# The new-state product of the second mixer from high and low parts, time-step tiles in shared places, and the streams' sums over their scaled x

## The chip, the cores and the metric

The kernel runs on one core of a Trainium2 chip. The metric is the device time of one execution in microseconds. Three runs of the kernel before gave a median of 2522.05 us (2519.87 to 2525.16).

## What is computed

One inference step of a two-layer streaming encoder in float32, for two groups of requests that share the weights: one new stream of 512 frames (the prompt) and 8 running streams of 16 frames each. Together these are 640 tokens of 1024 features. Layer 0 is a half-step feed-forward block, a mixer (S5 and attention) and a feed-forward block. Layer 1 is the same around a Mamba-2 mixer, the "second mixer", which is where the change is. Its core, from the reference:

```python
def step(h, inp):
    x_c, dt_c, b_c, c_c = inp
    cs = jnp.cumsum(dt_c * a, axis=1)
    seg = cs[:, :, None] - cs[:, None]
    decay = jnp.exp(jnp.where(causal, seg, -jnp.inf))
    cb = jnp.einsum('btgn,bsgn->btsg', c_c, b_c)
    w = cb[..., None] * decay * dt_c[:, None]
    y = jnp.einsum('btsgr,bsgrp->btgrp', w, x_c)
    y = y + jnp.einsum('btgn,bgrpn->btgrp', c_c, h) * jnp.exp(cs)[..., None]
    to_end = jnp.exp(cs[:, -1:] - cs) * dt_c
    h_new = h * jnp.exp(cs[:, -1])[..., None, None] + jnp.einsum('bsgr,bsgn,bsgrp->bgrpn', to_end, b_c, x_c)
    return h_new, y
```

There are 4 groups of 8 heads; a head has 64 values and a state of 64x128. The last einsum is the new-state product: over the tokens of a chunk, B (128 state columns) with x scaled by `to_end` (512 columns: 8 heads of 64). The result is gated by silu(z), normalised per group and multiplied by the output weights.

## The kernel before

The program runs six phases one after the other (two feed-forward blocks around each mixer). Nearly all large products are made from float32 weights that are split into two fp32r tiles, a high part (ScalarE, which the profile calls ACT, casts; L101) and a low part (VectorE, DVE, subtracts; L102), by the helper `split`. A product is then three fp32r matmuls, high·high, high·low and low·high (helper `mm3`, L148). Weights that are scaled too come from L127 and L128. A few small products of the mixers are plain F32 matmuls. A framework orders the instructions of each engine when the program is built, by priorities and by when tiles of its pools come free; the order on an engine is fixed from then on. Tiles of one name share `bufs` places in SBUF; a tile with a name takes the next place as soon as its last reader is done.

The second mixer holds the tokens in five chunks of 128: c = 0 to 3 for the prompt, c = 4 for the 8x16 stream tokens. It first computes the time steps (tiles `dt` and `cs`, 32 rows by 640 tokens; `cs` is written to `cs_d` in DRAM) and the first group's inputs. Then it goes through 20 steps (g, c), groups in order, c in the order 4, 0, 1, 2, 3. Around step i stand:

- `core_a` of step i + 1: loads `bx` (B, C and four blocks of x of one chunk, 384 KB, two places, L1682) and `csb` (L1687), builds the decays (`csb`, L1709 to L1717), the product C·B (L1713), transposes B (L1714, copied to `bk` by ACT at L1720) and x (L1723), and scales x twice per head: `xe` by `to_end` times dt (for the state) and `xd` by dt (for y). In group 3 `xd` comes from DVE (L1727), all else from ACT (L1731). For c = 4 it also splits `xe` and `bk` into high and low parts (into a place of the pool of `h0`, in group 0 into that of `og`, and into `bs`) and stores them to `xb_d`, for a later phase.
- `core_b` (c < 4): C times the old state (L1749), the new-state product `pst` from `bk` and `xe` (L1753, one F32 matmul of 128x512), the new state `hst` (L1759), the weighted sum (L1767, eight F32 matmuls, one for each head, from `xd` and `csb`), and y (L1771, L1772 and four instructions of L1774, which read `bx` last and so free its place). For c = 0 there is no old state.
- `core_s` (c = 4): the streams' sums (L1786), the streams' states `h0` (four loads of 512 KB for a group, L1478, four places) times C (L1791), and their sum over `xe` (L1793, L1794), which is transposed (L1797) and added to x (L1800).
- one or two fills: a projection with its convolution (`xbc`, L1600 to L1609) or a gate (`gate_in`, L1621 to L1627) of the next group, with 512 KB weight loads at L120; after the third group there are none left.
- `gate_out` of the group before: loads `zz` (L1815), gates (L1816), sums squares (L1820, L1821), normalises (L1823, L1824), splits into `og` and projects (L148 with `og`), adding to `yacc` (L1832).

In groups 0 to 2 the projections of the next group fill the engines between the steps. The last group's steps have none; after them comes the gate of group 3 with the normalisation. SP issues all these loads and stores in its own fixed order.

## Time and profile before

| | |
|---|---|
| median of three runs | 2522.05 us (2519.87 to 2525.16) |
| profiled execution, its own time | 2521.54 us |
| span of its trace | 2519.8 us |
| TensorE (PE) busy | 2480.4 us (98%) |
| DVE busy | 2013.5 us (80%) |
| ACT busy | 1269.7 us (50%) |
| POOL busy | 376.8 us (15%) |
| granted TensorE clock, mean | 0.999 |
| steps of the second mixer | about 1656 to 2046 us of the span |

A page line such as `L148 PE MATMUL bank<-w,og 128*128 128x512` names the source line, the engine, the operation, the tile written and the tiles read, and the shape. `bank` is a PSUM bank. A wait is written behind an instruction as `[1.71 <-DMA bx<-bcx_d]`: the engine stood idle for 1.71 us before it, until that transfer was in. An F32 matmul appears as two records; an fp32r matmul as one. Lines that issue a DMA carry the engine SPq, and the time there is that of the issue, not of the transfer. Starts are counted from the span's beginning.

### The profile page before, as it was taken

The page shows a single profiled execution, that of the slowest core. Times are in us where ns is not written, and L with a number is a line of the kernel's source. Part 1 is how long each engine was busy: PE and PEld are TensorE (multiplying, and loading weights), DVE is VectorE, ACT ScalarE, POOL GpSimd, SP SyncE. Part 2 cuts the span into 40 slices and gives each one's busy share as a digit, 9 for nine tenths or more (in the row PEclk, how much of TensorE's full clock was granted, in tenths as well). Part 3 has the DMA queues.
Part 4 walks back from the last instruction along what each step waited for, and adds up shares of the span by engine and source line. Part 5 has one row for each costly group of instructions (what it writes and reads, how often), then busy time and mean ns, then how long its engine had stood idle before and what let it go on. Part 6 is the DMA issues. An engine that isn't in the chain of part 4 may idle for free. (4 is left out here: it accounts for less than half of the span.)

```text
span 2519.8 us, 40822 instructions
## 1 busy us (share of the span) xinstructions
PE 2480.4 (98%) x15559; PEld 2278.3 (90%) x15559; DVE 2013.5 (80%) x3507; ACT 1269.7 (50%) x2390; POOL 376.8 (15%) x493
## 2 busy tenths in 40 slices
PE   9999999999999999999999999999999999999998
PEld 8999999878789999999999999998989879999897
DVE  8788777666879888877988887777576789998887
ACT  4443344336744555553455554566565543554542
POOL 0000001210130000013000002311121162111121
PEclk9999999999999999999999999999999999999999
DMA  5332335443221433462144434456464723555563
GB/s 187 109 101 86 108 118 156 145 154 122 79 84 59 121 101 99 111 165 66 59 114 113 121 101 132 152 163 210 139 215 135 244 74 100 159 147 166 150 174 116
DMA packets 178085, 324.80 MB, mean 129 GB/s; under 512 B 21296, under 2 KB 90928, under 8 KB 177376
## 3 DMA queue, kind: packets, MB, share of 16 engines
q1 hardware_dynamic: 164032, 293.83, 36.4%
q0 software_dynamic: 13856, 28.35, 5.8%
q8 instruction: 122, 2.00, 0.3%
q14 instruction: 75, 0.61, 0.1%
HBM read 259.56 MB, written 40.54 MB: 119 GB/s over the span
## 5 line engine op out<-in xcount | busy, mean ns | idle before, releaser
L101 ACT CAST w<-raw 128x512 fp32r<-128x512 f32 (+1 forms) x721 | 532.7, 769 | 333.9 <-DVE raw L370 145.1
L102 DVE TENSOR_TENSOR w<-raw,w 128x512 fp32r<-128x512 f32 (+2 forms) x721 | 621.3, 883 | 84.7 <-ACT w L101 81.6
L387 PE MATMUL bank<-xhi,w 128*128 128x320 f32 x2432 | 436.0, 309 | 2.2 <-DVE s L429 1.4
L387 PE MATMUL bank<-T,w 128*128 128x320 f32 x2736 | 428.0, 309 | 5.4 <-ACT bank L404 2.8
L387 PEld LDWEIGHTS bank<-T,w 128*128 128x128 f32 x2736 | 406.8, 188 | 8.4 <-ACT bank L404 5.3
L387 PEld LDWEIGHTS bank<-xhi,w 128*128 128x128 f32 x2432 | 376.8, 188 | 6.1 <-DVE s L429 2.2
L148 PE MATMUL bank<-xhi,w 128*128 128x256 f32 (+2 forms) x2272 | 361.3, 310 | 5.0 <-DVE yacc L1832 1.4
L148 PEld LDWEIGHTS bank<-xhi,w 128*128 128x128 f32 x2272 | 334.3, 187 | 15.0 <-issue 3.7
L148 PE MATMUL bank<-w,h 128*128 128x512 f32 (+1 forms) x1500 | 346.5, 389 | 0.2 <-DVE yacc L234 0.2
L148 PEld LDWEIGHTS bank<-w,h 128*128 128x128 f32 x1500 | 277.8, 188 | 57.6 <-ACT h L101 1.6
L387 PE MATMUL bank<-xlo,w 128*128 128x320 f32 x1216 | 227.7, 309 | 0.0
L370 DVE TENSOR_TENSOR raw<-raw 128x512 f32<-128x512 f32 x304 | 211.7, 696 | 3.4
L387 PEld LDWEIGHTS bank<-xlo,w 128*128 128x128 f32 x1216 | 190.7, 188 | 0.0
L148 PE MATMUL bank<-xlo,w 128*128 128x256 f32 (+2 forms) x1136 | 189.8, 308 | 0.0
L536 POOL DMA_DIRECT2D yacc<-ev x84 | 72.7, 890 | 690.7 <-ACT ev L535 608.8
L148 PEld LDWEIGHTS bank<-xlo,w 128*128 128x128 f32 x1136 | 170.9, 187 | 0.6
L523 PE MATMUL bank<-w,h 128*128 128x512 f32 x576 | 134.5, 389 | 0.0
L523 PEld LDWEIGHTS bank<-w,h 128*128 128x128 f32 x576 | 107.8, 188 | 22.8
L400 ACT COPY mx<-bank 128x320 f32<-128x320 f32 x152 | 64.5, 425 | 105.4 <-PE bank L387 105.0
L234 DVE SCALAR_TENSOR_TENSOR yacc<-bank,yacc 128x512 f32<-128x512 f32 x118 | 80.5, 686 | 39.6 <-PE bank L148 39.0
L532 DVE SCALAR_TENSOR_TENSOR yacc<-bank,yacc 128x512 f32<-128x512 f32 x84 | 57.7, 687 | 67.4 <-PE bank L523 67.4
L148 PE MATMUL bank<-w,og 128*128 128x512 f32 x432 | 103.0, 393 | 0.0
(442 smaller groups left out, 3352.0 us busy)
## 6 DMA issues: line engine op xcount, KB each, us to landing
raw<-in_w_gate_dram SPq DMA_DIRECT2D x88, 512.0 KB, 3.6
raw<-in_w_up_dram SPq DMA_DIRECT2D x88, 512.0 KB, 4.1
raw<-in_w_down_dram SPq DMA_DIRECT2D x88, 512.0 KB, 3.6
raw<-in_m_in_dram SPq DMA_DIRECT2D x52, 512.0 KB, 4.5
yacc<-ev POOLq DMA_DIRECT2D x84, 256.0 KB, 4.7
raw<-in_m_out_dram SPq DMA_DIRECT2D x24, 512.0 KB, 4.3
csb<-cs_d SPq DMA_DIRECT2D x20, 512.0 KB, 5.0
h<-in_ssd_h_dram SPq DMA_DIRECT2D x16, 512.0 KB, 6.4
```

What stands on the lines that cost most here:

```text
L101: nc.scalar.copy(hi, src)
L102: return nc.vector.tensor_tensor(lo, src, hi.bitcast(F32), op=ALU.subtract)
L148: state["pe"] = nc.tensor.matmul(ps, a, b, start=(k == 0), stop=(k == n - 1)).ins
L234: state["acc"] = nc.vector.scalar_tensor_tensor(ya, pb, scale, ya, op0=ALU.mult, op1=ALU.add).ins
L370: V.tensor_tensor(o, v, w, op=ALU.subtract)
L387: nc.tensor.matmul(ps, A[p][:, a, k * 128:k * 128 + 128], X[p][b][:, k, :], start=(first and n == 0), stop=(n == 11), skip_group_check=True)
L400: nc.scalar.copy(e[n], ps)
L523: nc.tensor.matmul(ps, a[:, u], b[:, v], start=(first and n == 0), stop=(n == 5), skip_group_check=True)
L532: V.scalar_tensor_tensor(ya, ps, 0.5 / ALPHA, ya, op0=ALU.mult, op1=ALU.add)
L536: nc.gpsimd.dma_start(yacc[:, t, 512 * j:512 * j + 512], e, accum_op=ALU.add)
```

## The change

It has four parts, all in the second mixer.

1. `core_a` makes high and low parts for every chunk. `bk` is split straight from PSUM (ACT cast, DVE subtract) in place of ACT's copy. x scaled by `to_end` goes into a new tile `xr` (one place) and is split into `xe`, now two fp32r halves. `core_b` then makes the new state from three fp32r matmuls (high·high, high·low, low·high).
2. For c = 4 the stores to `xb_d` read `xe` and `bk` directly. The separate splits and their places in `h0`, `og` and `bs` are gone.
3. `dt` now stands in the place of `og` and `cs` in one of `xe`.
4. `core_s` writes the streams' sums over `xd`, not `xe`.

Lines above L1720 keep their content and move by one (L1682 is L1683 in the new kernel, L1709 is L1710). L1727 becomes L1730. L1753 keeps its number.

```diff
@@ -1632,7 +1632,8 @@
             nc.sync.dma_start(dr[:, 0:256], I["m1_dt"])
             split(dtw[:, 0, 0:256], dtw[:, 1, 0:256], dr[:, 0:256])
             tok = wk.tile([128, NT, 3, 32], F32, name="tok")
-            dt, cs = (wk.tile([32, T], F32, name=n) for n in ("dt", "cs"))
+            dt = wk.tile([128, 4, 2, 128], F32, name="og", bufs=1).rearrange("p q k c -> p (q k c)")[:32, :T]
+            cs = wk.tile([128, 2, 512], F32, name="xe", bufs=2).rearrange("p a c -> p (a c)")[:32, :T]
             rst, te = (wk.tile([128, 1024], F32, name="csb", bufs=2)[:32, :T] for _ in range(2))
             with after_norm():
                 V.memset(rst, 1.0)
@@ -1716,28 +1717,26 @@
                 V.tensor_tensor(cbm, pcb[:, 0:128], mc[:, c // 4, :], op=ALU.mult)
                 V.tensor_tensor(csb, csb, cbm[:, None, :].to_broadcast([128, 8, 128]), op=ALU.mult)
 
-                bk = wk.tile([128, 128], F32, name="bk", bufs=2)
-                nc.scalar.copy(bk, pcb[:, 128:256])
+                bk = wk.tile([128, 2, 128], F32R, name="bk", bufs=2)
+                split(bk[:, 0], bk[:, 1], pcb[:, 128:256])
                 px = bank_b()
                 for q in range(4):
                     nc.tensor.transpose(px[:, 128 * q:128 * q + 128], xs[:, q], ident)
-                xd, xe = (wk.tile([128, 512], F32, name=n, bufs=2) for n in ("xd", "xe"))
-                for o, k in ((xe, 2), (xd, 1)):
+                xd = wk.tile([128, 512], F32, name="xd", bufs=2)
+                xr = wk.tile([128, 512], F32, name="xr", bufs=1)
+                xe = wk.tile([128, 2, 512], F32R, name="xe", bufs=2)
+                for o, k in ((xr, 2), (xd, 1)):
                     if g == 3 and k == 1:
                         V.tensor_tensor(by_head(o), by_head(px), tok[:, c, k, hs, None].to_broadcast(hb3), op=ALU.mult)
                     else:
                         for h in range(8):
                             d = slice(64 * h, 64 * h + 64)
                             nc.scalar.mul(o[:, d], px[:, d], tok[:, c, k, 8 * g + h:8 * g + h + 1])
+                    if k == 2:
+                        split(xe[:, 0], xe[:, 1], xr)
                 if c == 4:
-
-                    xs_ = (wk.tile([128, 2, 512], F32R, name="h0", bufs=4) if g else
-                           wk.tile([128, 4, 2, 128], F32R, name="og", bufs=1).rearrange("p (a q) k c -> p a (q k c)", a=2))
-                    bs_ = wk.tile([128, 2, 128], F32R, name="bs", bufs=1)
-                    split(xs_[:, 0], xs_[:, 1], xe)
-                    split(bs_[:, 0], bs_[:, 1], bk)
-                    nc.sync.dma_start(xb_d[g][:, :, 0:512].rearrange("a t c -> t a c"), xs_.bitcast(F32))
-                    nc.sync.dma_start(xb_d[g][:, :, 512:640].rearrange("a t c -> t a c"), bs_.bitcast(F32))
+                    nc.sync.dma_start(xb_d[g][:, :, 0:512].rearrange("a t c -> t a c"), xe.bitcast(F32))
+                    nc.sync.dma_start(xb_d[g][:, :, 512:640].rearrange("a t c -> t a c"), bk.bitcast(F32))
                 bl[g, c] = ct, xs, csb, el, ecs, bk, xd, xe
 
             def core_b(g, c):
@@ -1750,7 +1749,8 @@
                                          start=(q == 0), stop=(q == 3), skip_group_check=True)
 
                 pst = bank_b()
-                nc.tensor.matmul(pst, bk, xe, start=True, stop=True)
+                for n, (a, b) in enumerate(((0, 0), (0, 1), (1, 0))):
+                    nc.tensor.matmul(pst, bk[:, a], xe[:, b], start=(n == 0), stop=(n == 2))
                 hn = wk.tile([128, 512], F32, name="hst", bufs=2)
                 if c == 0:
                     nc.scalar.copy(hn, pst)
@@ -1777,7 +1777,7 @@
 
             def core_s(g, c):
 
-                ct, xs, csb, el, ecs, _, xd, xe = bl.pop((g, c))
+                ct, xs, csb, el, ecs, _, xd, _ = bl.pop((g, c))
                 c4 = ct.rearrange("p (j q i) -> p j q i", q=2, i=16)
                 for q in range(2):
                     G.tensor_copy(ctm[:, q, :, q, :], c4[:, :, q, :])
@@ -1790,11 +1790,11 @@
                     for q in range(2):
                         nc.tensor.matmul(pi[32 * j:32 * j + 32, :], ctm[:, q, j].rearrange("p q i -> p (q i)"),
                                          h0[:, q], start=(q == 0), stop=(q == 1), skip_group_check=True)
-                V.tensor_tensor(by_head(xe), by_head(pi), ecs[:, :, None].to_broadcast(hb3), op=ALU.mult)
-                V.tensor_tensor(xe, xe, pw, op=ALU.add)
+                V.tensor_tensor(by_head(xd), by_head(pi), ecs[:, :, None].to_broadcast(hb3), op=ALU.mult)
+                V.tensor_tensor(xd, xd, pw, op=ALU.add)
                 pt = bank_b().rearrange("p (q t) -> p q t", t=128)
                 for q in range(4):
-                    nc.tensor.transpose(pt[:, q, :], xe[:, 128 * q:128 * q + 128], ident)
+                    nc.tensor.transpose(pt[:, q, :], xd[:, 128 * q:128 * q + 128], ident)
                 y = wk.tile([128, 4, 128], F32, name="yb", bufs=6)
                 for q in range(4):
                     V.scalar_tensor_tensor(y[:, q, :], xs[:, q], chp[:, 0, 4 * g + q:4 * g + q + 1],
```

The change also moves instructions on the engines. Three places follow. The first is DVE between the step (0, 3), whose y is `yb`, and the step (1, 0), whose decays are the `csb` at the end; `hst` is the state of (0, 3), `acc` and `cvs` belong to a convolution, `w` to scaled output weights. Before:

```order
L1759 TENSOR_TENSOR hst_17439<-hst_17439,bank_17437 128x512
L1600 SCALAR_TENSOR_TENSOR acc_17370<-ext_17305,cw_15587,acc_17370 128x664
L1771 TENSOR_TENSOR yb_17452<-bank_17432,ecs_17164 128x512
L1600 SCALAR_TENSOR_TENSOR acc_17370<-ext_17305,cw_15587,acc_17370 128x664
L102 TENSOR_TENSOR h0_17424<-xe_17407,h0_17424 128x512
L102 TENSOR_TENSOR bs_17425<-bk_17399,bs_17425 128x128
L1772 TENSOR_TENSOR yb_17452<-yb_17452,bank_17443 128x512
L1605 SCALAR_TENSOR_TENSOR cvs_17376<-ext_17305,acc_17370 128x128
L1607 SCALAR_TENSOR_TENSOR acc_17370<-ext_17305,acc_17370 128x512
L1774 SCALAR_TENSOR_TENSOR yb_17452<-bx_17158,chp_15590,yb_17452 128x128 x4
L1709 TENSOR_TENSOR csb_17613<-csb_17613,tok_15609 128x1024
L128 SCALAR_TENSOR_TENSOR w_17783<-raw_17781,chp_15590,w_17783 128x512
```

After:

```order
L1759 TENSOR_TENSOR hst_17459<-hst_17459,bank_17455 128x512
L1600 SCALAR_TENSOR_TENSOR acc_17390<-ext_17325,cw_15587,acc_17390 128x664
L102 TENSOR_TENSOR xe_17429<-xr_17428,xe_17429 128x512
L1771 TENSOR_TENSOR yb_17472<-bank_17450,ecs_17178 128x512
L1605 SCALAR_TENSOR_TENSOR cvs_17396<-ext_17325,acc_17390 128x128
L1607 SCALAR_TENSOR_TENSOR acc_17390<-ext_17325,acc_17390 128x512
L1772 TENSOR_TENSOR yb_17472<-yb_17472,bank_17463 128x512
L1710 TENSOR_TENSOR csb_17633<-csb_17633,tok_15609 128x1024
L1774 SCALAR_TENSOR_TENSOR yb_17472<-bx_17172,chp_15590,yb_17472 128x128 x4
L128 SCALAR_TENSOR_TENSOR w_17807<-raw_17805,chp_15590,w_17807 128x512 x2
```

The subtract of the next step's `csb` now stands ahead of the four L1774 that end the step and release `bx`. One scaling of `w` has gone behind them (the two in the last row).

The second place is SP's queue of the same steps: `bx` with number 17611 (17631 after) is the load of step (1, 0), `out_ssd_p` the final state of group 0. Before:

```order
L1687 DMA csb_17613<-cs_d_15570 128x8x128
L1762 DMA out_ssd_p_dram<-hst_17439 128x512
L1478 DMA h0_17663<-in_ssd_h0_dram 128x2x512
L1478 DMA h0_17667<-in_ssd_h0_dram 128x2x512
L1609 DMA bcx_d2_15573<-cvs_17376 128x128
L1608 DMA bcx_d2_15573<-acc_17370 128x4x128
L1739 DMA xb_d1_15577<-h0_17424 128x2x512
L1740 DMA xb_d1_15577<-bs_17425 128x2x128
L1682 DMA bx_17611<-bcx_d1_15572 128x768
L1478 DMA h0_17671<-in_ssd_h0_dram 128x2x512
L1478 DMA h0_17675<-in_ssd_h0_dram 128x2x512
```

After:

```order
L1688 DMA csb_17633<-cs_d_15570 128x8x128
L1739 DMA xb_d1_15577<-bk_17419 128x2x128
L1762 DMA out_ssd_p_dram<-hst_17459 128x512
L1738 DMA xb_d1_15577<-xe_17429 128x2x512
L1608 DMA bcx_d2_15573<-acc_17390 128x4x128
L1609 DMA bcx_d2_15573<-cvs_17396 128x128
L1703 DMA ecs_17944<-cs_d_15570 64x4x128 x2
L1683 DMA bx_17631<-bcx_d1_15572 128x768
```

The four `h0` loads are gone from here, and the load of `bx` has the two `ecs` loads ahead of it and the stores of `xe` and `bk` further ahead. The `h0` loads of group 1 now stand in group 0's steps, right after the streams' step of group 0:

```order
L120 DMA raw_17480<-in_m1_in_dram 128x1024
L1688 DMA csb_16764<-cs_d_15570 128x8x128
L1478 DMA h0_17687<-in_ssd_h0_dram 128x2x512
L1478 DMA h0_17691<-in_ssd_h0_dram 128x2x512
L1478 DMA h0_17695<-in_ssd_h0_dram 128x2x512
L1608 DMA bcx_d1_15572<-acc_16523 128x4x128
L1609 DMA bcx_d1_15572<-cvs_16529 128x128
L1683 DMA bx_16762<-bcx_d0_15571 128x768
L1478 DMA h0_17699<-in_ssd_h0_dram 128x2x512
L120 DMA raw_17556<-in_m1_in_dram 128x1024
```

Three of them are ahead of the `bx` load of an early step of group 0, the fourth behind it.

The third place is PE in group 3's steps (the tail), from the projection of a chunk of group 2 (`og`) over step (3, 1) to the next; `bx` and `ident` at L1713 to L1723 are of step (3, 2), which is prepared meanwhile. Before:

```order
L148 MATMUL bank<-w,og 128x512 x24
L1713 MATMUL bank<-bx 128x128
L1714 MATMUL bank<-ident,bx 128x128
L1723 MATMUL bank<-ident,bx 128x128 x4
L1749 MATMUL bank<-bx,hst 128x128 x4
L1753 MATMUL bank<-xe,bk 128x512
L1767 MATMUL bank<-csb,xd 64x128 x8
L1821 MATMUL bank<-ones,zz 128x2
L148 MATMUL bank<-w,og 128x512 x8
L1753 MATMUL bank<-xe,bk 128x512
L148 MATMUL bank<-w,og 128x512 x16
L1713 MATMUL bank<-bx 128x128
```

After:

```order
L148 MATMUL bank<-w,og 128x512 x24
L1767 MATMUL bank<-csb,xd 64x128 x7
L1714 MATMUL bank<-bx 128x128
L1715 MATMUL bank<-ident,bx 128x128
L1724 MATMUL bank<-ident,bx 128x128 x4
L1748 MATMUL bank<-bx,hst 128x128 x4
L1753 MATMUL bank<-xe,bk 128x512 x3
L1767 MATMUL bank<-csb,xd 64x128
L1821 MATMUL bank<-ones,zz 128x2
L148 MATMUL bank<-w,og 128x512 x24
L1753 MATMUL bank<-xe,bk 128x512 x3
L148 MATMUL bank<-w,og 128x512 x2
```

Seven of the eight L1767 of the step now run before the instructions on the next step's `bx` (L1714 and on), and the projection's 24 matmuls are no longer cut by the new-state product of the next step.

## The prediction

> **What bounds the kernel now.** I read the page first, then a table by stage of the second mixer, the waits of TensorE there, and the timelines of PE, DVE and SP at the places where it waits.
>
> The page's engine line, and the stage table (columns: the stretch, its us, then each engine's busy us with its instructions, the granted clock, the DMA share and GB/s):
>
> ```profile
> PE 2480.4 (98%) x15559; PEld 2278.3 (90%) x15559; DVE 2013.5 (80%) x3507; ACT 1269.7 (50%) x2390; POOL 376.8 (15%) x493
> ```
>
> ```profile
> 1656.00:1737.00 81.00, 81.00 (x594) 76.46 (x593) 58.77 (x96) 55.29 (x159) 12.03 (x33) 1.00 0.55 166
> 1737.00:1754.00 17.00, 15.59 (x114) 14.57 (x112) 16.06 (x27) 13.19 (x36) 3.12 (x8) 1.00 0.75 239
> 1780.00:2003.00 223.00, 222.89 (x1466) 202.59 (x1465) 149.89 (x261) 125.92 (x328) 42.05 (x67) 1.00 0.57 183
> 2003.00:2046.00 43.00, 39.18 (x229) 29.95 (x229) 37.17 (x66) 23.28 (x57) 17.29 (x21) 1.00 0.42 131
> ```
>
> TensorE has no idle time in two long stretches (81.00 of 81.00 us, 222.89 of 223.00), at full granted clock: there the time is the sum of its matmuls, and DVE (73% and 67% busy) and ACT are beside the path. Two short stretches differ. In 1737–1754 DVE is busy 16.06 of 17 us, in the tail 2003–2046 (the last group's steps, without projections between them) 37.17 of 43. There a later DVE can hold TensorE up. What it waits for, first in 1640–2003, then from 2003 on (total us, times, longest):
>
> ```profile
> PE bank L1713 <- DMA bx<-bcx_d: 1.7, 1, 1.7
> ...
> PE bank L1713 <- DMA bx<-bcx_d: 1.6, 2, 1.0
> PE bank L1767 <- DVE xd L1727: 0.9, 1, 0.9
> PE bank L1821 <- POOL zz L1820: 0.7, 1, 0.7
> ```
>
> So the change can act in three ways: by the matmuls it shortens, by one wait of 1.7 us in the bulk, and by 3.2 us of waits in the tail (1.6 + 0.9 + 0.7).
>
> **(a) The new-state product.** One F32 matmul of 128x512 becomes three in fp32r, in 16 steps. Three pieces of PE's timeline (start, us, line; an F32 matmul is recorded as two):
>
> ```profile
> 1684.03 1.02 PE L1753 MATMUL bank<-xe,bk 128*128 128x512 f32 x2
> 1684.99 1.09 PE L1767 MATMUL bank<-csb,xd 128*64 128x128 f32 x16
> ...
> 2012.74 1.06 PE L1749 MATMUL bank<-bx,hst 128*128 128x128 f32 x8
> 2013.63 1.02 PE L1753 MATMUL bank<-xe,bk 128*128 128x512 f32 x2
> ...
> 2024.02 1.06 PE L1749 MATMUL bank<-bx,hst 128*128 128x128 f32 x8
> 2025.01 1.09 PE L1767 MATMUL bank<-csb,xd 128*64 128x128 f32 x16
> ...
> 2028.39 5.73 PE L148 MATMUL bank<-w,og 128*128 128x512 f32 x24
> 2033.96 1.05 PE L1749 MATMUL bank<-bx,hst 128*128 128x128 f32 x8
> ```
>
> From the product's start to the next instruction's is 1684.99 − 1684.03 = 0.96 us. The instruction behind it, L1767, costs 0.10 to enter: L1749 lasts 2013.63 − 2012.74 = 0.89 when the product follows and 2025.01 − 2024.02 = 0.99 when L1767 does. Three fp32r matmuls of the same shape cost 3 × (2033.96 − 2028.39)/24 = 3 × 0.232 = 0.70, with the entry 0.80. The saving is 0.96 − 0.80 = 0.16: 16 × 0.16 = **−2.6 us**. No row shows fp32r ahead of L1767. If there is no entry cost any more the saving is 0.26 (−4.2); if leaving and entering cost another 0.10, it is 0.06 (−1.0).
>
> The Trainium skill says on "FP8 and Floating Point Precision", TensorE Precision Notes, that true FP32 takes four passes through the array (H·H, H·L, L·H, L·L). By that, with the trace's own 0.232 for a pass, the product would be 0.93 and three passes 0.70: an estimate of 16 × −0.23 = −3.7; the trace's 0.96 − 0.10 = 0.86 says a little under four passes, and I keep to it.
>
> What is added on the other engines, from the rows of the splits that exist for c = 4 (count, min/median/max ns):
>
> ```profile
> L101 ACT CAST h<-xe x3: 672/762/763, 1743.5 to 1964.0; 128x512 fp32r<-128x512 f32 x3
> L102 DVE TENSOR_TENSOR h<-xe,h x3: 679/681/693, 1745.0 to 1964.7; 128x512 fp32r<-128x512 f32 x3
> ...
> L102 DVE TENSOR_TENSOR bs<-bk,bs x4: 282/284/285, 1664.2 to 1965.3; 128x128 fp32r<-128x128 f32 x4
> ```
>
> Sixteen steps gain 0.68 + 0.28 = 0.96 us of DVE (15.4 in all) and 0.76 of ACT (12.2). In the bulk (12 of the 16) PE hides them: DVE has 22 us free in the first long stretch and 73 in the second. Only the tail's four steps can feel them; (d) has them.
>
> **(b) The earlier h0 loads.** The streams' matmuls with h0, in groups 1 and 2:
>
> ```profile
> 1756.96 2.64 PE L1791 MATMUL bank<-h,ctm 128*32 128x512 f32 x16
> ...
> 1868.66 1.94 PE L1791 MATMUL bank<-h,ctm 128*32 128x512 f32 x16
> ```
>
> Group 1 takes 2.64 − 1.94 = 0.70 longer, since its last two tiles are still coming. After the change no split sits in their slots; SP issues them in group 0's steps, as soon as that group's own tiles are read. **−0.7 us** (0 if PE's 0.70 has another cause). Three of them now stand ahead of one load of bx in the first long stretch; PE waits for nothing there (81.00 of 81.00), so I take no cost; the bound is one slow issue, the 1.32 us of the SP row in (c).
>
> **(c) The one wait of the bulk.** PE waits at 1754 for bx of step (1,0). PE, then SP's issues, then DVE, whose L1774 is the last reader of the slot that this load takes; last, the landing of the 20 bx loads:
>
> ```profile
> 1754.30 0.46 PE L1713 MATMUL bank<-bx 128*128 128x128 f32 x2 [1.71 <-DMA bx<-bcx_d]
> ...
> 1748.35 0.69 SPq L1740 DMA_DIRECT2D xb_d<-bs  x1
> 1749.13 1.32 SPq L1682 DMA_DIRECT2D bx<-bcx_d  x1
> 1750.50 2.74 SPq L1478 DMA_DIRECT2D h<-in_ssd_h_dram  x2
> ...
> 1747.23 1.13 DVE L1774 SCALAR_TENSOR_TENSOR yb<-bx,chp,yb 128x128 f32<-128x128 f32 x4
> 1748.28 1.22 DVE L1709 TENSOR_TENSOR csb<-csb,tok 128x1024 f32<-128x1024 f32 x1
> 1749.42 1.41 DVE L128 SCALAR_TENSOR_TENSOR w<-raw,chp,w 128x512 fp32r<-128x512 f32 x2
> ...
> DMA to landing us min/median/max: 3.0/4.5/5.9
> ```
>
> L1774 ends at 1748.36, and SP issues bx at 1749.13, behind the store L1740; it takes 1.32 to issue and lands near 1754.2, 5.1 later, among h0 loads. By the order after, L1710's subtract (1749.42 − 1748.28 = 1.14) now stands ahead of L1774, and one weight scaling (half of 1.32) has gone behind it: L1774 ends 0.5 later, at 1748.8. The stores are out by then and the h0 loads gone, so bx goes out at 1748.9 and lands 4.5 later, at 1753.4. PE, ready at 1754.30 − 1.71 = 1752.59, waits 0.8: **−0.9 us**. With the shortest landing (3.0) the wait goes, −1.7; with the longest (5.9) it grows by 0.5.
>
> **(d) The tail.** PE's waits there, and the two issues behind the first two:
>
> ```profile
> 2011.89 0.46 PE L1713 MATMUL bank<-bx 128*128 128x128 f32 x2 [1.04 <-DMA bx<-bcx_d]
> 2023.15 0.49 PE L1713 MATMUL bank<-bx 128*128 128x128 f32 x2 [0.56 <-DMA bx<-bcx_d]
> 2027.02 0.43 PE L1767 MATMUL bank<-csb,xd 128*64 128x128 f32 x2 [0.92 <-DVE xd L1727]
> 2028.15 0.38 PE L1821 MATMUL bank<-ones,zz 128*128 128x2 f32 x2 [0.70 <-POOL zz L1820]
> ```
>
> First bx wait: step (3,0)'s L1774 now has the two new subtracts ahead of it, so bx is 0.96 later. Seven of step (3,1)'s eight L1767 matmuls have been moved ahead of it (the eight, 16 records, last 1.09 in the rows of (a); seven 0.95), work that is gone from behind it: net 0. Second: DVE starts that step 0.96 later, and ahead of (3,1)'s L1774 stand another 0.96 and L1710's 1.14, together 3.1; of this DVE's idle time (43.00 − 37.17 = 5.8 us over the tail) takes a part, I say 1.0: +2.1. PE then comes 2.1 later to where it waited for xd (L1727) and zz; by the order after, the L1767 that waited stands behind the next projection too: −0.92 − 0.70 = −1.6. Net **+0.5 us**, between −1.6 (DVE's idle time takes all the subtracts, and only xd's and zz's waits go) and +3.1 (none of it, and they stay).
>
> **Sum.** −2.6 − 0.7 − 0.9 + 0.5 = −3.7. The profiled execution took 2521.54 us (its span of 2519.8 and 1.7 around it), 0.51 under the median of 2522.05. So a profiled 2517.8, and **2518.3** on the median's scale. What a measurement can tell from no change is 0.2%, 5.0 us: faster means under 2517.0, slower over 2527.1. By the bounds of the terms the likeliest case lies between 2515.0 and 2521.0, with a third of it below 2517.0.
>
> **Rivals.**
>
> *B: only the matmuls count.* The h0 loads move, but bx waits as long (its landing is what it is, 5.1 among the weight loads that still fill 239 GB/s), and L1791's 0.70 stays. Then (a) + (d) = −2.1: 2519.9. For it: at 1737–1754 the DMA share is 0.75. Against: the issue itself took 1.32, in a queue of h0 loads.
>
> *C: slower, the splits hold DVE in the tail.* DVE takes its instructions in order, and a split's subtract waits for ACT's cast. The trace has that once:
>
> ```profile
> 1662.73 0.69 DVE L102 TENSOR_TENSOR og<-xe,og 128x512 fp32r<-128x512 f32 x1 [0.67 <-ACT og L101]
> ```
>
> DVE stood 0.67 there, with the next step's work behind it. In the tail the same stand, for both splits of four steps, with the work itself, is 4 × (0.96 + 2 × 0.67) = 9.2 us. If DVE sets the pace and its idle 5.83 us cannot take any of it, and the bulk gives 12 × 0.16 + 0.7 = 2.6, the kernel is 6.6 slower: 2528.6. It decides the sign as soon as more than 2.6 us of the 9.2 show. For it: DVE at 86% in the tail. Against: the casts' operands are ready early on an ACT that is busy 23.28 of 43 us. The Trainium skill has the mechanism as a rule on "TensorE: Matmul & The Clock Gate", Architectural detail: ACT and DVE are strictly first in, first out, only TensorE's queue can pull weight loads ahead. The 0.67 us row agrees with it.
>
> *D: the tail's waits go as well.* The reordered PE queue could fill all four (3.2 us) instead of the +0.5 above: 2518.3 − 3.7 = 2514.6, and with (a) near its upper bound 2513. For it: the seven moved matmuls. Against: bx still waits for L1774 behind more DVE work.
>
> *E: the change doesn't do what it says,* the three products run at the F32 rate: 3 × 0.86 in place of one adds 16 × 1.7 = 27 us, 2549. L148's 24 matmuls in 5.57 us speak against it.
>
> **Chances.** Likeliest case 0.46 (0.15 of it faster, 0.31 the same), B 0.18 (the same), D 0.16 (faster), C 0.19 (0.17 slower, 0.02 the same), E 0.01 (slower). Faster 0.15 + 0.16 = 0.31; the same 0.31 + 0.18 + 0.02 = 0.51; slower 0.18. A range that leaves out C's slow part and E holds 0.82: from D with (a)'s bound, 2513.0, to 2524.5, where half of C's price shows and bx at 1754 lands at its latest (4.6 − 2.6 + 0.5 = +2.5).
>
> **What would show it.** In the profile after: L1753 as 48 matmuls, and some 0.80 us from the first to L1767 (right for (a)); L1791 at 1.94 in group 1 (b); the wait at L1714 between 0 and 1.7 in 1737–1760 (c); PE idle in the tail near 4 us of some 43 (d). Wrong: PE idle anywhere else in the bulk; DVE waiting for L101 at L102 with PE idle behind it (C); L1753's three taking 0.96 or more.

## The result, and the profile after

The changed kernel takes 2519.22 us (median of 21 runs, 2517.19 to 2523.43), against 2522.01 us for the kernel before (21 runs beside it, 2519.79 to 2527.55): 2.8 us less, a ratio of 0.9987 with a 95% interval of 0.9981 to 0.9993. That is 1.8 to 4.8 us, clear of zero, but under the 5.0 us that I had set as "faster". The forecast was 2518.3 us. The profiled execution took 2517.19 us, the lowest of the 21, so its span (2515.5 us) shows more gain, 4.3 us, than the median does.

The page after, its engine line:

```profile
PE 2477.6 (98%) x15575; PEld 2279.0 (91%) x15575; DVE 2025.7 (81%) x3539; ACT 1275.3 (51%) x2402; POOL 373.4 (15%) x493
```

PE is busy for 2.8 us less though it has 16 records more, DVE has gained 12.2 and ACT 5.6. What PE waits for after the change, from the mixer's start to 2003 and then in the tail (total us, times, longest):

```profile
PE bank L1797 <- DVE xd L1794: 2.2, 1, 2.2
...
PE bank L148 <- DVE og L102: 1.1, 1, 1.1
PE bank L148 <- ACT og L101: 1.0, 1, 1.0
PE bank L148 <- ACT w L127: 0.7, 1, 0.7
PE bank L1821 <- DVE bk L102: 0.6, 1, 0.6
```

The wait for bx in the bulk (1.7 us before) is gone, and one of 2.2 us stands a few us further on, at the transposes of the streams' sums. In the tail the waits for bx, xd and zz (1.6, 0.9, 0.7) are gone, and waits for og and bk (2.1 and 0.6; `og` is the gated y in two parts, `bk` the transposed B) are there. (The wait for w was 0.6 before.)

The product in the timeline of PE, before and after (step (2, 1)), then the h0 matmuls after (step (1, 4)):

```profile
1914.63 1.06 PE L1749 MATMUL bank<-bx,hst 128*128 128x128 f32 x8
1915.52 1.02 PE L1753 MATMUL bank<-xe,bk 128*128 128x512 f32 x2
1916.47 1.09 PE L1767 MATMUL bank<-csb,xd 128*64 128x128 f32 x16
...
1911.84 1.06 PE L1748 MATMUL bank<-bx,hst 128*128 128x128 f32 x8
1912.66 0.95 PE L1753 MATMUL bank<-xe,bk 128*128 128x512 f32 x3
1913.54 1.09 PE L1767 MATMUL bank<-csb,xd 128*64 128x128 f32 x16
...
1751.46 0.38 PE L1714 MATMUL bank<-bx 128*128 128x128 f32 x2
...
1754.05 1.94 PE L1791 MATMUL bank<-h,ctm 128*32 128x512 f32 x16
```

From the start of the matmuls on `hst` to that of L1767 it is 1.84 us before (1916.47 − 1914.63) and 1.70 after (1913.54 − 1911.84). L1791 is at 1.94, as in the other groups.

The load of bx that PE waited for before, with the last reader of its place, after the change:

```profile
1745.67 1.13 DVE L1774 SCALAR_TENSOR_TENSOR yb<-bx,chp,yb 128x128 f32<-128x128 f32 x4
...
1746.83 0.34 SPq L1683 DMA_DIRECT2D bx<-bcx_d  x1
```

It goes out 4.63 us before the matmuls on bx (1751.46) and lands in 3.7 us; before, it went out 3.46 us before PE was ready for them (1752.59 − 1749.13) and took 5.0.

**The new wait, read through three engines.** PE, DVE, and ACT of the changed kernel around 1762:

```profile
1761.54 0.34 PE L148 MATMUL bank<-xlo,w 128*128 128x384 f32 x1
1764.09 0.65 PE L1797 MATMUL bank<-ident,xd 128*128 128x128 f32 x4 [2.22 <-DVE xd L1794]
```

```profile
1759.89 0.68 DVE L1793 TENSOR_TENSOR xd<-bank,ecs 128x512 f32<-128x512 f32 x1
1760.49 0.68 DVE L102 TENSOR_TENSOR w<-raw,w 128x512 fp32r<-128x512 f32 x1
1762.54 0.29 DVE L1605 SCALAR_TENSOR_TENSOR cvs<-ext,acc 128x128 f32<-128x128 f32 x1 [1.38 <-ACT ext L1602]
1762.75 0.68 DVE L1607 SCALAR_TENSOR_TENSOR acc<-ext,acc 128x512 f32<-128x512 f32 x1
1763.36 0.68 DVE L1794 TENSOR_TENSOR xd<-xd,bank 128x512 f32<-128x512 f32 x1
```

```profile
1761.65 0.22 ACT L1693 ACTIVATE el<-csb 128x8 f32<-128x8 f32 x1 [1.56 <-DMA csb<-cs_d]
1761.77 0.74 ACT L1602 ACTIVATE ext<-acc 128x664 f32<-128x664 f32 x1
```

The sum over xd (L1794) has all that it needs, but on DVE it stands behind L1605, which waits for a tanh (L1602) that on ACT stands behind L1693, which waits for a load of csb for a later step. None of these is an operand of the sum. In the kernel before, the same two instructions of DVE stood the other way round, and the longer stand at L1605 (2.94 us) hurt nobody:

```profile
1761.07 0.68 DVE L1794 TENSOR_TENSOR xe<-xe,bank 128x512 f32<-128x512 f32 x1
...
1765.28 0.29 DVE L1605 SCALAR_TENSOR_TENSOR cvs<-ext,acc 128x128 f32<-128x128 f32 x1 [2.94 <-ACT ext L1602]
```

The second mixer in stretches, in us between the starts on PE of the first matmul on bx of steps (0, 4), (1, 4), (1, 1), (3, 1) and of group 3's first gate matmul with ext, from the profiled executions (before: 1656.65, 1734.91, 1779.79, 2002.15, 2042.62). The stretches hold three, one, eight and four of the products. The kernels of the experiments stand here too.

| kernel | (0,4) to (1,4) | to (1,1) | to (3,1) | tail | sum | ratio to before, timed |
|---|---|---|---|---|---|---|
| before | 78.26 | 44.88 | 222.37 | 40.47 | 385.97 | 1 |
| changed | 77.89 | 44.58 | 219.98 | 39.99 | 382.44 | 0.9987 (0.9981–0.9993) |
| changed, again | 77.98 | 44.01 | 220.92 | 40.76 | 383.67 | 0.9989 (0.9980–0.9998) |
| e1_held | 77.89 | 43.37 | 222.66 | 40.06 | 383.98 | 0.9986 (0.9977–0.9994) |
| e2_f32hi | 78.44 | 48.18 | 221.68 | 44.67 | 392.96 | 1.0024 (1.0014–1.0033) |
| e3_f32 | 78.21 | 44.15 | 221.73 | 40.73 | 384.83 | 0.9991 (0.9982–0.9999) |
| e4_sumfirst | 77.81 | 42.79 | 220.85 | 41.15 | 382.60 | 0.9977 (0.9968–0.9986) |
| the same, again | 77.91 | 42.89 | 220.27 | 40.42 | 381.50 | 0.9978 (0.9969–0.9987) |
| e9_dt | 78.21 | 44.64 | 221.81 | 40.67 | 385.33 | 1.0009 (1.0000–1.0018) |
| e7_ogfirst | 77.90 | 46.12 | 220.10 | 43.38 | 387.51 | 0.9999 (0.9990–1.0008) |
| e8_both | 77.98 | 42.78 | 220.59 | 42.94 | 384.29 | 0.9985 (0.9977–0.9994) |
| e5_pool | 77.89 | 46.64 | 221.29 | 40.28 | 386.11 | 0.9988 (0.9979–0.9997) |
| f2_slots | 77.87 | 43.07 | 220.07 | 44.73 | 385.74 | 0.9997 (0.9989–1.0006) |
| f3_slots_og | 77.98 | 43.35 | 220.21 | 40.72 | 382.26 | 0.9998 (0.9989–1.0007) |

Executions of one program differ by about 1 us in these stretches, and those of the table by up to 3 us ahead of them; so the table is read for single waits, and the ratios for the time.

### The profile page after: what moved, and what is told of

Its sections match the earlier page's. It is cut to its first block, busy times and chain, and to the rows that moved or that the text cites. A ratio compares the mean times of both kernels' runs of the same rounds, so it can differ in the third digit from the quotient of the medians.

```text
span 2515.5 us, 40891 instructions
## 1 busy us (share of the span) xinstructions
PE 2477.6 (98%) x15575; PEld 2279.0 (91%) x15575; DVE 2025.7 (81%) x3539; ACT 1275.3 (51%) x2402; POOL 373.4 (15%) x493
## 5 line engine op out<-in xcount | busy, mean ns | idle before, releaser
L102 DVE TENSOR_TENSOR w<-raw,w 128x512 fp32r<-128x512 f32 (+2 forms) x721 | 621.4, 883 | 83.5 <-ACT w L101 80.5
```

Of the source, the lines that this page charges most:

```text
L102: return nc.vector.tensor_tensor(lo, src, hi.bitcast(F32), op=ALU.subtract)
```

## The experiments

My theory after the result: the products pay what the sum said, the wait for bx goes, and the 2.2 us wait for the sums, made by the order on DVE, takes nearly as much back; in the tail waits only change their names. The rivals are in the expectations.

**The changed kernel once more**, to see how far its profile repeats.

> The changed kernel as it is, on the chip of the next three runs, as their measure. Both theories: a span of 2515.5 us in the profile (as before in its first profile), a ratio to the kernel before of 0.9987 within 0.0006.

Ratio 0.9989 (0.9980 to 0.9998), span 2519.5 us. The ratio repeats, the span does not: 2.1 us of the 4.0 were lost before step (0, 4). In the mixer the wait for the sums is there again (1.6 us and 0.5 in group 3), PE waits 0.6 us for bx in group 0 and 1.2 in the tail. Of the 2.1 us lost early, about 1.1 fall near 666 us, where the granted clock is 0.50 from 666.4 to 669.8 in this execution and 1.00 in the first profile; 0.6 are the wait for bx. So the four us of the first profile are one execution's, and the 2.8 of the median are the result.

**Late h0 loads again.**

```diff
-                xe = wk.tile([128, 2, 512], F32R, name="xe", bufs=2)
+                held = c == 4 and g
+                xe = wk.tile([128, 2, 512], F32R, name="h0" if held else "xe", bufs=4 if held else 2)
```

> For the streams' chunk of groups 1 to 3, xe takes a place of h0's pool, as the separate split did before the change; all else is the changed kernel. The h0 loads are late again, and in DVE's order the sum over xd (the second of its two instructions) stands ahead of the convolution's last two. Theory 1 (the earlier loads save 2.4 us, but the new wait of 2.2 us for that sum gives them back): the wait for bx at step (1, 0) is back at about 1.7 us, L1791's matmuls of group 1 take 2.6 us, the 2.2 us wait at the transposes of xd is gone, and the span is within 0.6 us of the changed kernel's 2515.5. Theory 2 (the loads are worth their 2.4 us and the wait for the sum comes from the added subtracts, whatever the order): both waits are there, the span is 2517.5 or more.

The timeline of PE in step (1, 4) of this kernel:

```profile
1752.06 0.46 PE L1714 MATMUL bank<-bx 128*128 128x128 f32 x2 [0.20 <-DVE acc L1600]
...
1754.73 2.31 PE L1792 MATMUL bank<-h,ctm 128*32 128x512 f32 x16
...
1762.30 0.65 PE L1798 MATMUL bank<-ident,xd 128*128 128x128 f32 x4 [0.23 <-DVE xd L1795]
```

The matmuls on h0 are slower again (2.31, not 1.94), and with the sum ahead of L1605 in the order its wait is 0.23 us: as theory 1 said. But it also said that bx would wait 1.7 us again, and the wait at L1714 is 0.20. The load goes out at 1747.30, right behind its L1774 and 4.56 us before PE is ready for it, not 3.46 as in the kernel before; its landing is slow again, 4.6 us. So two things make this wait, when the load goes out and how long it takes, and late h0 loads set only the second. The traces agree on it: with the h0 loads beside it this load lands in 5.0 (before), 4.9 (e9_dt) and 4.6 us (this run), and with the early ones in 2.9 to 3.7 (the changed kernel twice, and all other runs).

The stretch to (1, 1) is 1.2 us shorter than the changed kernel's, the next 2.7 longer, with a new wait of 1.8 us for zz in group 2. The time, 0.9986, is that of the changed kernel. As the wait for the sums went and one for zz came, it doesn't tell what the loads alone are worth.

**One F32 product of the high parts.** The low parts are left out of the product, all else stays.

```diff
-                for n, (a, b) in enumerate(((0, 0), (0, 1), (1, 0))):
-                    nc.tensor.matmul(pst, bk[:, a], xe[:, b], start=(n == 0), stop=(n == 2))
+                nc.tensor.matmul(pst, bk[:, 0].bitcast(F32), xe[:, 0].bitcast(F32), start=True, stop=True)
```

> The changed kernel with one F32 matmul of the two high parts in place of the three fp32r ones; the splits stay, the low parts are left out of the product. Theory 1 (TensorE pays 0.22 to 0.25 us more for each of the 16 F32 products, and nothing hides it): the span is 3.5 to 4.0 us above the changed kernel's, 2519.0 to 2519.5, and PE's start of step (3, 1) is about 3 us later. Theory 2 (the product saves only the 0.16 us that I worked out, and the rest of the 3.3 us up to step (3, 1) is from the loads): 2.6 us above, 2518.1.

It takes 2529.15 us, 8.7 us more than the changed kernel beside it: far over both theories. Where the steps have no wait, the price is as worked out: in the first stretch 0.46 to 0.55 us above the changed kernel for three products, 0.15 to 0.18 each, and from the matmuls on bx of step (2, 2) to those of (2, 3), one product and no wait, 23.47 us (1918.67 to 1942.14) against 23.31 (1911.08 to 1934.39), 0.16. The rest is two waits, and what follows them. Its windows of 1764 to 1772 around the first (us, then busy us of PE, PEld, DVE, ACT and POOL, granted clock):

```profile
1764.40:1767.60 3.20, 0.01 (x1) 0.00 (x0) 2.67 (x6) 1.31 (x5) 0.25 (x2) 0.82 1.01 359
1767.60:1769.00 1.40, 1.36 (x6) 1.36 (x7) 1.33 (x2) 0.19 (x1) 0.00 (x0) 0.50 1.05 381
1769.00:1772.00 3.00, 3.00 (x12) 3.00 (x11) 1.03 (x5) 2.26 (x4) 0.00 (x0) 0.50 0.88 250
```

PE stands still for 3.23 us (the same wait for the sum as in the changed kernel, longer by 1.0, with the same order on DVE; the stand at L1605 is only 0.53 us of it, as DVE comes there later), and then the granted clock is 0.50 until 1773.3, at which eight matmuls of 384 columns take 2.76 us in place of 1.55. A wait of 3.4 us for zz in the tail is followed by the same. So this kernel told the product's price only in its undisturbed steps.

**Everything but the first part of the change.** For c < 4 no splits, one F32 product of the full values.

```diff
-                split(bk[:, 0], bk[:, 1], pcb[:, 128:256])
+                if c == 4:
+                    split(bk[:, 0], bk[:, 1], pcb[:, 128:256])
+                else:
+                    nc.scalar.copy(bk[:, 0].bitcast(F32), pcb[:, 128:256])
...
-                xr = wk.tile([128, 512], F32, name="xr", bufs=1)
                 xe = wk.tile([128, 2, 512], F32R, name="xe", bufs=2)
+                xr = wk.tile([128, 512], F32, name="xr", bufs=1) if c == 4 else xe[:, 0].bitcast(F32)
...
-                    if k == 2:
+                    if k == 2 and c == 4:
```

(The product is that of the last diff.)

> The changed kernel without its first part: for c < 4 neither B nor the scaled x is split, and the new state is one F32 matmul of the full values, as before the change; the loads of h0 stay early, dt and cs stay in shared places, the streams' sums over xd. The order puts the sum over xd ahead of the convolution. Theory 1 (the early loads free the wait for bx and L1791, 2.4 us, and the products are worth 0.15 each beside it): against the kernel before, 2.4 us from step (1, 4) to step (1, 1), nothing in the tail, the ratio 0.9988 to 0.9991. Theory 2 (the wait for bx went in the changed kernel because DVE's order was another one, not by the loads): the wait for bx stays at 1 us or more, only L1791's 0.7 us goes, the ratio 0.9995 or more.

Ratio 0.9991 (0.9982 to 0.9999). The waits of PE up to 2003:

```profile
PE bank L1799 <- DVE xd L1796: 0.9, 1, 0.9
...
PE bank L1714 <- DMA bx<-bcx_d: 0.5, 1, 0.5
```

Between the theories: bx waits 0.5 us (1.2 less than before), L1791's 0.7 goes, and a wait of 0.9 for the sums comes, here too, although the order has it ahead of L1605: there are 26 matmuls of the projection between L1793 (the h0 matmuls here) and the transposes, and 41 in the changed kernel. The bx row speaks for the loads: SP issues bx only 2.93 us before PE is ready for it (1751.45, 1754.38), later than in the kernel before (3.46), and yet the wait is shorter, since it lands in 3.3 us and not in 5.0. From step (1, 4) to (1, 1) that is 0.73 us less (44.15 against 44.88), 0.7 + 1.2 − 0.9 = 1.0 being expected of it. The tail is 0.3 longer than before, with all its old waits. The interval overlaps the changed kernel's (0.9987): what the first part adds is told by its rows, not by the time. (The third stretch is 0.8 to 1.75 us longer than the changed kernel's two, for eight products.)

**The sum first.** One edge of order: in step (1, 4), DVE does the sum ahead of the convolution's last two (`cvt` is what `xbc` put there last).

```diff
-                V.tensor_tensor(xd, xd, pw, op=ALU.add)
+                add = V.tensor_tensor(xd, xd, pw, op=ALU.add)
+                if g == 1:
+                    for i_ in state["cvt"]:
+                        tc.add_manual_dep(i_.ins, add.ins.name,
+                                          mybir.DependencyInfo(mybir.DependencyClass.NoSync, mybir.DependencyReason.DATA),
+                                          reason="sum first")
```

> The changed kernel with one edge of order in step (1, 4): on DVE the sum over xd goes ahead of the last two instructions of the convolution that stands there (they wait for ACT). Nothing is computed differently. Theory 1 (the 2.2 us wait is made by that order alone): the wait goes, and the span falls by 2.0 to 2.4 us, to 2513.3. Theory 2 (it is the next limit, some chain through ACT and the csb load that PE reaches anyway): a wait of over 1 us stands at the next place, at L1821 for zz or at bx of step (1, 1), and the span falls by less than 1 us.

DVE, then PE of this kernel:

```profile
1761.38 0.68 DVE L102 TENSOR_TENSOR w<-raw,w 128x512 fp32r<-128x512 f32 x1
1761.98 0.67 DVE L1795 TENSOR_TENSOR xd<-xd,bank 128x512 f32<-128x512 f32 x1
1762.58 0.28 DVE L1605 SCALAR_TENSOR_TENSOR cvs<-ext,acc 128x128 f32<-128x128 f32 x1
```

```profile
1762.71 0.66 PE L1803 MATMUL bank<-ident,xd 128*128 128x128 f32 x4 [0.56 <-DVE xd L1795]
```

The wait falls from 2.2 us to 0.56, and nothing stands in its place: the stretch to (1, 1) is 42.79 us (44.58 and 44.01 in the changed kernel's two profiles), 1.2 to 1.8 less. The tail of this execution is 1.2 longer, with a wait of 1.7 us for bx that the changed kernel's second profile has too (1.2). Timed, 0.9977 (0.9968 to 0.9986), the best so far. Theory 1 for the wait, with 0.5 us left of it. The span, 2516.4 us, did not fall to the 2513.3 that it gave; it is 3.1 under that of the changed kernel's second profile and 0.9 over the first.

**The same once more.**

> The kernel with the one edge of order in step (1, 4) once more, to tell whether it beats both. Theory 1 (the edge takes away a wait of 1.6 to 2.9 us, after which the granted clock can fall too): ratio to the kernel before 0.9972 to 0.9982, no wait over 0.8 us before the tail, the granted clock 1.00 throughout the second mixer. Theory 2 (its first result lay low by chance): 0.9985 or more, as the changed kernel has it.

Ratio 0.9978 (0.9969 to 0.9987), 2518.52 us against 2523.85. Its longest wait before the tail is 0.7 us, and the granted clock is 1.00 throughout: theory 1. This version beats the kernel before in both runs; that it beats the changed kernel too is likely (0.9987 and 0.9989 there; beside the first of the two runs 2520.45 us against 2518.56, 1.9 us), but the intervals of the ratios overlap.

**The low part of og first in the tail**, by the same kind of edge.

```diff
-                split(og[:, :, 0], og[:, :, 1], y)
+                og_lo = split(og[:, :, 0], og[:, :, 1], y)
+                for i_ in state.pop("late3", ()):
+                    tc.add_manual_dep(i_.ins, og_lo.ins.name,
+                                      mybir.DependencyInfo(mybir.DependencyClass.NoSync, mybir.DependencyReason.DATA),
+                                      reason="og first")
```

(`late3` holds the next step's subtract of xe's low part and its product for xd.)

> The changed kernel with an edge of order in the last group's steps: on DVE the subtract that makes the low part of og goes ahead of the next step's two that make xd and the low part of x. Nothing is computed differently. Theory 1 (in the tail DVE's order makes PE wait 1.1 us for og's low part): that wait falls under 0.3 us, nothing of its size takes its place, and PE's time from step (3, 1) to the gate of group 3 falls by 0.8 to 1.2 us. Theory 2 (DVE's work sets the tail's length, in whatever order): another wait of about 1 us stands in its place, and the time changes by less than 0.4 us.

The waits of PE from 2000 on:

```profile
PE bank L1714 <- DMA bx<-bcx_d: 2.6, 2, 2.3
```

Both waits for og (1.1 and 1.0) are gone, and one of 2.3 us for bx has come. The load of bx hasn't moved: it goes out right behind L1774 (2022.36 + 1.14), 19.7 us after the tail's first matmul, as in the changed kernel (19.6). PE, freed of the waits for og, only comes to it earlier. Two windows, around the wait and behind it:

```profile
2024.00:2027.00 3.00, 0.65 (x4) 0.31 (x3) 2.62 (x5) 1.97 (x4) 0.19 (x1) 1.00 0.47 131
2028.10:2034.90 6.80, 6.80 (x32) 5.47 (x31) 5.30 (x9) 3.11 (x11) 3.46 (x4) 0.50 0.26 76
```

Again the clock falls, to 0.50 for 6.8 us. The tail is 43.38 us long, 2.6 to 3.4 more, and all of that comes behind the wait: from the matmuls on bx to the tail's end it is 20.54 us (2026.69 to 2047.23), and 16.95 in the changed kernel (2021.69 to 2038.64). The ratio is 0.9999 (0.9990 to 1.0008). Theory 2, and worse: two waits of 1 us that are made one of 2.3 cost more than they did. In the bulk, where the order is the changed kernel's, the wait for the sums was 2.15 us and the clock fell behind it too, which makes the stretch 46.12 us.

**Both edges.**

> Both edges of order, that of step (1, 4) and that of the last group's steps. Theory 1 (waits of the order, each by itself): the gains add, 1.5 to 2 us in step (1, 4) and about 1 us in the tail, a ratio to the kernel before of 0.9970 to 0.9978. Theory 2: no better than with the first edge alone, 0.9977 or more.

0.9985 (0.9977 to 0.9994), not better than the first edge alone (0.9977 and 0.9978; the intervals overlap): theory 2. The gain in step (1, 4) is there (42.78 us), the tail is 42.94, with 4.0 us of waits for bx (1.6 and 2.4) and the granted clock at 0.50 for 3.4 us behind the second.

**bx out of L1774's hands.** The loads of steps (3, 2) and (3, 3) go to places of h0's pool, once with the first edge, once with both.

```diff
-                bx = wk.tile([128, 6, 128], F32, name="bx", bufs=2)
+                if g == 3 and c in (2, 3):
+                    bx = wk.tile([128, 2, 512], F32, name="h0", bufs=4).rearrange("p a b -> p (a b)")[:, :768]
+                    bx = bx.rearrange("p (u t) -> p u t", t=128)
+                else:
+                    bx = wk.tile([128, 6, 128], F32, name="bx", bufs=2)
```

> The changed kernel with the order edge of step (1, 4), and with bx of steps (3, 2) and (3, 3) loaded into places of h0's pool, which are free by then, so that these loads don't wait for L1774. Theory 1 (in the tail PE waits for bx because its place is released late by DVE): both waits for bx go, the transposes of step (3, 3) run two steps early, and the time from step (3, 1) to the gate of group 3 falls by 1 to 2.5 us against the kernel with the first edge alone (41.2 us there); ratio to the kernel before 0.9968 to 0.9974. Theory 2 (DVE's sum of work in the tail is the bound, whatever PE waits for): waits for xd, og or zz of the same total take their place; less than 0.5 us.

> As the last, with the edge that puts og's low part first in the last group's steps. Theory 1: with bx out of DVE's hands, the og waits of 1.1 and 1.0 us go too; the time from step (3, 1) to the gate of group 3 is 2 to 4 us under the 41.2 us of the kernel with the first edge alone; ratio 0.9962 to 0.9970. Theory 2 (DVE's work is the bound): no better than the last run.

The waits of PE in the tail, of the one and of the other:

```profile
PE bank L1831 <- ACT csb L101: 2.9, 1, 2.9
PE bank L1772 <- DVE hst L1764: 1.8, 1, 1.8
PE bank L1831 <- POOL zz L1830: 1.3, 1, 1.3
```

```profile
PE bank L1831 <- POOL zz L1830: 5.2, 2, 4.2
```

The waits for bx are gone, and others on ACT, DVE and POOL stand there, 6.0 and 5.2 us, with the granted clock at 0.50 for some 6.8 us behind the longest of each; the tails are 44.73 and 40.72 us long. Ratios 0.9997 (0.9989 to 1.0006) and 0.9998 (0.9989 to 1.0007), although the gain in step (1, 4) is in both. The outcome is theory 2's, other waits in place of the old. That DVE's work sets when they end is argued and not shown: the lowered clock is in both tails, and the longest waits are put down to ACT and POOL.

**The low part of x on POOL** in the last group.

```diff
-                            split(xe[:, 0], xe[:, 1], xr)
+                        if g == 3 and c < 4:
+                            nc.scalar.copy(xe[:, 0], xr)
+                            G.tensor_tensor(xe[:, 1], xr, xe[:, 0].bitcast(F32), op=ALU.subtract)
+                        else:
+                            split(xe[:, 0], xe[:, 1], xr)
```

> The changed kernel with the low part of x made by POOL in place of DVE in the last group's four steps. Theory 1 (in the tail the added subtracts hold L1774 and with it the place of bx, and og's low part): DVE's tail loses 4 times 0.68 us, bx of steps (3, 2) and (3, 3) goes out some 0.7 to 1.4 us earlier, and PE's time from step (3, 1) to the gate of group 3 falls by 0.5 to 1.5 us. Theory 2 (other work, the decays and the gate, sets the tail): it changes by less than 0.3 us either way, or grows, as POOL takes longer for the subtract.

The tail is 40.28 us, between the changed kernel's 39.99 and 40.76, with waits of 0.6 to 0.9 us for zz, csb and bx. Ratio 0.9988 (0.9979 to 0.9997). That is theory 2's number, but the run doesn't test theory 1: DVE was not relieved. It is busy for 37.34 of the 40.28 us, more than with the subtracts (36.14 and 35.69 in the changed kernel's profiles), since its own instructions take longer beside POOL's:

```profile
2018.37 1.29 POOL L1738 TENSOR_TENSOR xe<-xr,xe 128x512 fp32r<-128x512 f32 x1
...
2018.47 1.74 DVE L102 TENSOR_TENSOR og<-yb,og 128x512 fp32r<-128x512 f32 x1
```

In the changed kernel this L102 takes 0.67 us (at 2014.73). In the bulk, whose order is the changed kernel's, the wait for the sums was 2.9 us this time, and the clock behind it 0.73 and 0.70 in two windows of 3 us.

**dt in og's place, alone**, in the kernel before.

```diff
-            dt, cs = (wk.tile([32, T], F32, name=n) for n in ("dt", "cs"))
+            dt = wk.tile([128, 4, 2, 128], F32, name="og", bufs=1).rearrange("p q k c -> p (q k c)")[:32, :T]
+            cs = wk.tile([32, T], F32, name="cs")
```

> The kernel before with one piece of the change: dt in the place of og. Theory 1 (the projections of the second mixer, 3 us of the bulk's 3 us gain not explained by products and waits apart, run 1 to 3 per cent faster in all changed kernels since the tiles lie elsewhere in SBUF): L148's matmuls of 384 columns take about 174 ns from start to start in place of 177, those with og 233 in place of 227, about 0.1 us a step, a ratio of 0.9995 to 0.9999. Theory 2 (it is not where the tiles lie): the same 177 and 227 ns as in the kernel before, ratio 1.0000 within 0.0006.

The projections behind the product of step (2, 1) in three kernels, in PE's timeline: before, changed, and this one.

```profile
1920.43 2.99 PE L148 MATMUL bank<-xhi,w 128*128 128x384 f32 x16
...
1924.81 5.71 PE L148 MATMUL bank<-w,og 128*128 128x512 f32 x24
```

```profile
1917.40 2.93 PE L148 MATMUL bank<-xhi,w 128*128 128x384 f32 x16
...
1921.69 5.84 PE L148 MATMUL bank<-w,og 128*128 128x512 f32 x24
```

```profile
1922.85 2.93 PE L148 MATMUL bank<-xhi,w 128*128 128x384 f32 x16
...
1927.14 5.84 PE L148 MATMUL bank<-w,og 128*128 128x512 f32 x24
```

Sixteen matmuls of 384 columns take 2.99 us before and 2.93 in the other two, 4 ns less each; 24 of 512 columns 5.71 and 5.84, 5 ns more each. Their operands and shapes are the same in all three; giving one other tile the place of og did it in the last. (No trace shows where tiles lie in SBUF, so whether their own operands moved with it is open.) The third stretch is 0.56 us shorter here than before. The time was not shorter, 1.0009 (1.0000 to 1.0018): the matmuls on bx wait twice, 1.7 and 1.6 us, where the kernel before waits once, 1.7. Theory 1 by the rows, not by the time.

## Why the prediction was right, step by step

The forecast of −3.7 us met −2.8 (1.8 to 4.8), and the mechanism named first, the products on a busy PE, holds. That the number came so near is in part luck: a wait of 2.2 us that I didn't see stood against 0.8 us more at bx than I had taken, and 0.6 of pace that is not in the sum.

- **(a) The products: right in size, with the parts not where I put them.** 0.16 us each was forecast, and 0.14 came (1.84 to 1.70), 16 × 0.14 = 2.2 against 2.6. Against kernels with an F32 product in its place (e2_f32hi) it is 0.15 to 0.18. From the product to L1767 it is 0.88 us, not 0.80: if the three matmuls take 0.70, the entry to L1767 costs 0.18 and not 0.10 (an estimate). So the product itself saves only 0.07 (0.95 to 0.88), and the other 0.07 comes ahead of it, where L1748 takes 0.82 to the product in place of 0.89, which the sum didn't have. Four passes for F32, which would have made 0.23 each, did not show.
- **(b) The h0 loads: right in the row.** L1791 went from 2.64 to 1.94 us, and with late loads it was 2.31 (e1_held). What that is worth in the time, no run tells alone.
- **(c) The wait for bx: right that it shrinks, half right in why.** 0.9 was forecast; all of the 1.7 went, in both profiles. The traffic did more than I had said: without the h0 loads bx lands in 3.7 us, and I had 4.5. The step on DVE had the wrong sign: I had L1774 end 0.5 us later, and it ended at 1746.80, 4.66 us ahead of the matmuls on bx against 4.23 before, with no store in front of bx any more (issued 0.03 us after L1774, 0.77 before). Either part alone leaves a rest: 0.20 with late loads (e1_held), 0.5 with a late L1774 (e3_f32).
- **What I did not see: the wait for the streams' sums, +2.2 us.** PE idle elsewhere in the bulk was my own sign of being wrong. I asked what is late next behind bx and looked only at bx. The order after had L1794 behind L1605 and L1607, whose wait for ACT's tanh was in the trace before, 2.94 us long and harmless there. e4_sumfirst shows it: one edge takes 1.2 to 1.8 us off this stretch.
- **What no row of before showed: the projections' pace, −0.6 us.** It comes with another layout of tiles (e9_dt, 0.56 us over the third stretch).
- **(d) The tail: near in size by luck, wrong in its parts.** +0.5 was forecast beside the four products' −0.6; the tail went by −0.5 and +0.3 in two profiles, so +0.1 and +0.9 beside them. The waits for xd and zz went, as I had it; that for bx, which I had grow by 2.1, went too (or is 1.2, in the second profile), and those for og, 2.1 us, were not in my working. Rival C, that DVE holds the tail, did not come in the change itself. Its mechanism shows in one place: in e7_ogfirst bx goes out no earlier than in the changed kernel, right behind DVE's L1774, and PE waits there for what it saved at og. For the whole tail it stays argued: e8_both, f2_slots and f3_slots_og lose what they gain, but part of that is the lowered clock. DVE is busy for 34.31 of the tail's 40.47 us before and 36.14 of 39.98 after, by the windows:

```profile
2002.15:2042.62 40.47, 37.24 (x222) 28.62 (x222) 34.31 (x62) 20.55 (x52) 17.29 (x21) 1.00 0.42 132
```

```profile
1998.66:2038.64 39.98, 37.18 (x226) 29.38 (x226) 36.14 (x67) 21.40 (x55) 15.87 (x20) 1.00 0.43 134
```

The sum from the first profile: −2.2 (products) − 0.7 (h0) − 1.7 (bx) + 2.2 (sums) − 0.6 (projections) + 0.1 (tail) = −2.9; the table has 382.44 − 385.97 = −3.5, so 0.6 us is not accounted for. Some 0.4 of it lies in one step: from the matmuls on bx of (2, 0) to those of (2, 1) it is 25.12 us before (1866.07 to 1891.19), 24.64 after (1864.02 to 1888.66) and 25.05 in e9_dt, with the matmuls on zz 0.3 us sooner behind the projection after the change. What stays open beside that: why the layout of tiles changes the matmuls' pace, and why single waits for bx differ by 1 us between executions of one program.

## What to carry to other kernels

When a wait is taken away on an engine that is busy all the time, read on each in-order queue what now stands ahead of the next thing that it waits for; an instruction that waited there before without harm is the first suspect, and one edge of order can be worth nearly as much as the change (some 2 us against 2.8 here). Where a second engine is nearly as busy as the first, as DVE in this tail, moving its work about renamed the first one's waits in all five runs that tried. Several short waits are better than one long one, since the clock can fall behind the long one.

## What was not expected of the hardware

- The granted clock falls to 0.50 for 3.4 or 6.8 us behind single waits of PE of 2.15 and 2.35 (e7_ogfirst), 2.40 (e8_both), 2.88 (e5_pool), 2.89 (f2_slots), 3.23 and 3.41 (e2_f32hi) and 4.19 us (f3_slots_og). The work behind the wait then took 2.1 (e8_both, 19.10 us to the tail's end against 16.96 in e4_sumfirst) and 3.6 us longer (e7_ogfirst, above). Behind the 2.22 us of the changed kernel it stayed at 1.00 (1764 to 1772).
- It is not the wait's length alone that decides. Within a trace these stretches start whole multiples of 3.413 us apart (e7_ogfirst: 1768.68 and 2028.09, 76 times). With each of the fourteen traces cut into windows on that grid, the clock fell behind every window in which PE was busy for up to 0.428 of it, and behind none of the some 10,000 in which it was busy for 0.429 or more. The 2.15 us of e7_ogfirst lay in one window, the 2.22 of the changed kernel across two (e7_ogfirst's window and the next, then the changed kernel's):

```profile
1765.27:1768.68 3.41, 1.26 (x9) 0.94 (x9) 2.69 (x5) 1.23 (x4) 0.30 (x2) 1.00 1.04 389
1768.68:1772.09 3.41, 3.41 (x12) 3.12 (x11) 1.35 (x6) 2.80 (x5) 0.87 (x3) 0.50 0.87 228
...
1760.07:1763.49 3.42, 1.80 (x11) 1.48 (x9) 2.04 (x5) 1.25 (x5) 0.00 (x0) 1.00 1.00 350
```

  The grid lies elsewhere against the program in each execution, so a wait of a little over 2 us can cost its length alone in one execution and some 2 us on top in the next. The Trainium skill says on "TensorE: Matmul & The Clock Gate", What's actually happening, that the clock is halved after at least one idle window of about 3.4 us that runs free of the program. The length and the free run agree with these traces; but a window with PE busy for 0.41 of it (e7_ogfirst, behind the wait of 2.35 us) was enough, so it need not be idle, and the runs decide.
- Three fp32r matmuls of 128x512 save 0.14 to 0.18 us over one in F32 between the same neighbours (1.70 against 1.84 us, and e2_f32hi). By an estimate from the rows, 0.96 us to the next start less 0.10 of entry, the F32 one takes 0.86 us, 3.7 times the 0.232 of one fp32r matmul.
- Matmuls of one shape ran 2% faster (0.06 us in 2.99, 384 columns) or 2% slower (0.13 in 5.71, 512 columns) when a tile that they don't read was put elsewhere (e9_dt); whether that moved their operands too, no trace shows.
- An instruction of DVE can take more than twice its time beside one of POOL: L102 on og 1.74 us beside POOL's subtract (e5_pool), 0.67 in the changed kernel.
